# Up products of the gated layers as 512-column matmuls, and a quarter of their low weight parts by an adding transfer

## The chip, the cores and the metric

The kernel runs on one core of one Trainium2 chip. The metric is device time in microseconds (us), from the start to the end of one execution. A core has a matrix engine (TensorE, "PE" in the profile), whose weight loads the profile lists apart as "PEld", a vector engine (VectorE, "DVE"), a scalar engine (ScalarE, "ACT"), a general engine (GpSimd, "POOL") and SyncE ("SP"), which here only issues transfers. Each takes its instructions strictly in the order in which they were written, and an instruction that waits holds up all those behind it on its engine.

## The reference

The model has four layers of attention with a convolved, gated feed-forward part ("gated layers" here), and then one layer of another kind with two SwiGLU parts. All data are float32, 256 tokens of width 1024. The change touches the feed-forward part of the four layers:

```python
D_FF = 2752
CONV_W = 3

def conv_gated_ffn(h, w_up, conv_w, conv_b, w_down):
    u = h @ w_up
    C = u.shape[-1]
    u = lax.conv_general_dilated(u, conv_w[:, None, :].astype(u.dtype), window_strides=(1,),
                                 padding=[(CONV_W - 1, 0)], dimension_numbers=('NWC', 'WIO', 'NWC'),
                                 feature_group_count=C) + conv_b
    gate, val = jnp.split(u, 2, axis=-1)
    return (jax.nn.silu(gate) * val) @ w_down

for layer in range(DEPTH):
...
    h = rmsnorm(x, ffn_norm[layer])
    x = x + conv_gated_ffn(h, ffn_w_up[layer], ffn_conv_w[layer], ffn_conv_b[layer], ffn_w_down[layer])
```

## The kernel before

**Products.** Each float32 operand is split into a high part (the value rounded to float32r) and a low part (the rest), and a product is the sum of high x high, high x low and low x high. Activations lie feature-major, 128 features by 256 tokens, with both parts side by side in one tile (`act.hl`). `fm` (L191) runs over blocks of 128 x 128 weights. In its plain form a block is three matmuls of 256 columns (weight high by activation high, weight high by activation low, weight low by activation high), all summed in one half of a PSUM bank. In its wide form (`wide=True`) it is two: weight high by both activation parts as 512 columns, which fills a whole bank with two sums, and weight low by activation high as 256 columns. Whoever reads a wide result has to add the two halves.

**Weights.** They come in 282 chunks of 1 MB (`dma_to`, L128, on SP's queue, four `stage` buffers). A chunk is two units of 8 blocks. `split_next` (L152) makes the parts of a unit: ACT copies it to `whi` (L164), rounding, and DVE subtracts `whi` from the staged weights into `wlo` (L167), 128 x 1024 elements each. Both have five buffers. When PE's order reaches the fifth block of unit u, `take` (L170) has unit u + 4 split; the DVE instruction of it is written six blocks later, in these layers (`self.lag = 6`, `self.AHEAD = 4`). So `wlo` of a unit is written 22 blocks ahead of its first use.

**Order.** Nothing is scheduled by time. `tick` (L230) is called after each block and lets helpers (generators, `spawn`) write their next instructions once the block count (`self.pos`) has passed the number that they asked for. So the place of every ACT and DVE instruction is fixed by block counts, and the engines meet through semaphores.

**A gated layer** (`ffn_layer`, L767) multiplies 43 column tiles up, 8 blocks each: 21 pairs (a gate tile and its value tile) and one single tile that holds the two halves of the last 64 columns. The first pair and the single tile go together, and then 20 pairs follow, one after the other. Both tiles of a pair lie in one PSUM bank `u` (three of these; five others, `s`, serve attention). When a pair is done, `gate` (L788) is started for it. It writes, in this order: DVE multiplies both tiles by the norm factor `r` into `ub` (L792, 128 x 512); two blocks on, ACT starts both convolution sums `y` (L798); two on, DVE adds two taps of the first (L802); one on, ACT takes SiLU `gs` (L269) and DVE adds the taps of the second; four on, DVE multiplies to `g` (L814), ACT rounds it to `ghl` (L818); four on, DVE writes the low part (L825). All of that for one pair is written while PE's order is in the next pair, together with the splits of two units. The first gates wait for `r`, which comes only after the first blocks. The down product (22 units, wide) follows in the same order of the gated tiles.

The wide form with the adding of halves is what the SwiGLU parts use already (`swiglu`, L862, gate instructions L882 to L899): ACT copies the second halves (L882), DVE adds the first halves (L885), then DVE multiplies by `r` (L888).

Of the kernel before, what the change touches and what calls it, by code (L numbers as in the profile page):

```python
# [12 lines left out]
AF = mybir.ActivationFunctionType  # L13
OP = mybir.AluOpType
# [4 lines left out]
P = 128  # L19
T = 256  # L20
D = 1024
KT = 8
# [51 lines left out]
def up_cols(i):  # L74
    if i < 21:
        return [np.arange(128 * i, 128 * i + 128), np.arange(D_FF + 128 * i, D_FF + 128 * i + 128)]
    a = np.arange(128 * 21, D_FF)
    return [np.concatenate([a, D_FF + a])]
# [8 lines left out]
class Act:  # L87
# [3 lines left out]
    def __init__(self, hl, stacked=None):  # L91
        self.hl, self.h, self.l, self.done, self.stacked = hl, hl[:, 0], hl[:, 1], set(), stacked


class Net:
    def __init__(self, tc, ctx, A):
        self.tc = tc
        self.nc = tc.nc
        self.A = A
        self.side = []  # L100
        self.made = {}
        pool = lambda n, b, **k: ctx.enter_context(tc.tile_pool(name=n, bufs=b, **k))
        self.const = pool("const", 1)
        self.res = pool("res", 1)
        self.stage = pool("stage", 4)
        self.wsp = pool("wsp", 5)
        self.tmp = pool("tmp", 2)
        self.pu = pool("pu", 3, space=PSUM)
        self.psd = pool("psd", 5, space=PSUM)
        self.dram = pool("dram", 1, space=DRAM)  # L110
        self.rec = []
        self.pos = 0
        self.n_dma = 0
        self.n_split = 0
        self.chunks = {}
        self.wunits = {}
        self.AHEAD = 3
        self.acc = {}
        self.summed = {}
        self.late = None  # L120
        self.bt_bufs = 3
        self.lag = LAG[0]
        self.v_at = 5
# [29 lines left out]
    def split_next(self, step, lag=0):  # L153

        nc = self.nc
        i = self.n_split
        src = self.chunks[i // 2][:, (i % 2) * 1024:(i % 2) * 1024 + 1024]
        hi = self.wsp.tile([P, 1024], F32R, tag="whi", name="whi")
        lo = self.wsp.tile([P, 1024], F32R, tag="wlo", name="wlo")
        self.wunits[i] = (hi, lo)  # L160
        self.n_split += 1
        for o in range(0, 1024, step):
            s = slice(o, o + step)
            nc.scalar.activation(hi[:, s], src[:, s], AF.Copy)  # L164
            if lag:
                yield lag
            nc.vector.tensor_tensor(lo[:, s], src[:, s], hi[:, s].bitcast(F32), OP.subtract)  # L167
            yield 0
# [595 lines left out]
    def ffn_layer(self, layer, xf, nxt):  # L764
        nc = self.nc
        name = "ffn_w_up"
        cv = lambda i, part, tap: self.vec[:, CONV_COL + ((layer * 4 + tap) * N_UP + 2 * i + part):][:, 0:1]  # L767
        with ExitStack() as st:
            pool = st.enter_context(self.tc.tile_pool(name="ffn%d" % layer, bufs=2))
            gp = st.enter_context(self.tc.tile_pool(name="ffng%d" % layer, bufs=1))  # L770
            ga = Act(gp.tile([P, 2, 22, T], F32R, tag="ghl", name="ghl"), 21)
            gh, gl = ga.h, ga.l
            gz = gl[:, 21]
            self.zero(gz[64:])
            ub = [gp.tile([P, 2, 258], F32, tag="ub%d" % i, name="ub%d" % i) for i in range(3)]
            for t in ub:
                nc.gpsimd.memset(t[:, :, 0:2], 0.0)
            self.lag = 6
            self.AHEAD = 4
            self.start_norm(delay=27)  # L780
            order = [0, 21] + list(range(1, 21))
            lead = [up_cols(0), up_cols(21)]
            banks = [self.ubank(), self.ubank()]

            def gate(n, i, bank):

                np_ = len(up_cols(i))
                m = P if np_ == 2 else 64  # L788
                while self.r is None:
                    yield 1  # L790
                u = ub[n % 3]
                nc.vector.tensor_tensor(  # L792
                    u[:, 0:np_, 2:258], bank[:, 0:np_ * T].rearrange("p (a t) -> p a t", t=T),
                    self.r.unsqueeze(1).to_broadcast([P, np_, T]), OP.mult)
                yield 2
                y = pool.tile([P, 2, T], F32, tag="y", name="y")
                for p in range(np_):
                    nc.scalar.activation(y[:, p], u[:, p, 2:258], AF.Identity, scale=cv(i, p, 2), bias=cv(i, p, 3))  # L798

                def taps(p):  # L800
                    for tap in (1, 0):
                        nc.vector.scalar_tensor_tensor(y[:, p], u[:, p, tap:tap + T], cv(i, p, tap), y[:, p],  # L802
                                                       op0=OP.mult, op1=OP.add)
                yield 2
                taps(0)
                yield 1
                gs = pool.tile([P, T], F32, tag="gs", name="gs")
                self.silu(gs[:m], y[:m, 0])
                if np_ == 2:
                    taps(1)  # L810
                yield 4
                g = pool.tile([P, T], F32, tag="g", name="g")
                if np_ == 2:
                    nc.vector.tensor_tensor(g, gs, y[:, 1], OP.mult)  # L814
                else:
                    nc.scalar.activation(g[:64], y[64:128, 0], AF.Copy)
                    nc.vector.tensor_tensor(g[:64], gs[:64], g[:64], OP.mult)
                nc.scalar.activation(gh[:m, i], g[:m], AF.Copy)  # L818
                if np_ == 1:
                    nc.scalar.activation(gz[:64], g[:64], AF.Copy)  # L820
                if n == 21:
                    self.pin()
                yield 4
                low = gl[:, i] if np_ == 2 else gh[64:, i]
                nc.vector.tensor_tensor(low, g[:m], gh[:m, i].bitcast(F32), OP.subtract)  # L825
                ga.done.add(i)

            def start(n, i, bank, delay=0):
                gen = gate(n, i, bank)
                self.spawn(gen, delay or next(gen), ga)  # L830

            self.fm([(b[:, p * T:p * T + T], name, layer, cols, p == 0)
                     for b, parts in zip(banks, lead) for p, cols in enumerate(parts)], xf, range(KT))
            for n, i in enumerate(order):
                if n >= 2:
                    bank = self.ubank()
                    for p, cols in enumerate(up_cols(i)):
                        self.fm([(bank[:, p * T:p * T + T], name, layer, cols, True)], xf, range(KT))
                    start(n, i, bank)
                else:  # L840
                    start(n, i, banks[n], 8 * n)
            xn = self.new_act()
            rows = [np.arange(128 * kt, 128 * kt + 128) for kt in range(21)]
            rows.append(np.tile(np.arange(128 * 21, D_FF), 2))

            def after(c, ps):
                for n in range(2):
                    nc.vector.tensor_tensor(self.x[:, c], self.x[:, c], ps[:, n], OP.add)  # L848
                nxt(xn, c)

            self.down("ffn_w_down", layer, ga, order, after, rows)
            self.lag = 4
        return xn
# [607 lines left out]
```

## Time and profile before

| | us |
|---|---|
| median of 2 runs (1761.38 to 1761.99) | 1761.68 |
| profiled execution, its own time | 1761.36 |
| its span, first to last instruction | 1759.6 |
| PE busy | 1742.1 (99%) |
| DVE busy | 1404.4 (80%) |
| ACT busy | 1118.0 (64%) |
| POOL busy | 27.4 (2%) |

The profile is of one execution. Its own time stands 1.8 us above its span, and 0.3 us below the median. Busy time is a mean over stages; PE's counts pipelined matmuls with modelled ends, so 99% does not say that PE ran at its peak. The granted clock of TensorE over the whole is 0.995 of 2.4 GHz. The four gated layers' up products take about 124 us each.

### The profile page before, as it was taken

To read this page: it belongs to the slowest core of one execution; us is meant where nothing else is said; L and a number is where in the kernel's file an instruction comes from. 1 tells how busy PE (TensorE), PEld (TensorE's weight loads), DVE (VectorE), ACT (ScalarE), POOL (GpSimd) and SP (SyncE) were. 2 spreads that over 40 slices of the span, in tenths; PEclk is the share of its full clock that TensorE was granted. 3 is DMA by queue.
4 is the path that set the end of the run, shared out by engine and by line. 5 is a ranking of instruction groups with operands and counts; after the bars stand their busy time and mean duration, and the time that the engine had idled before them with its cause. 6 is when DMAs were issued, how large, how long until landed. Compare 5 with 4: busy or idle time off the path is not lost.

```text
span 1759.6 us, 31591 instructions
## 1 busy us (share of the span) xinstructions
PE 1742.1 (99%) x12556; PEld 1635.2 (93%) x12556; DVE 1404.4 (80%) x2582; ACT 1118.0 (64%) x1996; POOL 27.4 (2%) x67
## 2 busy tenths in 40 slices
PE   9999999999999999999999999999999999999998
PEld 8999998999999899999899999988888999988886
DVE  6989996897998688899689799868875767568763
ACT  6776664676766477666467766656655557466553
POOL 1000000000000000000000000000000020000000
PEclk9999999999999999999999999999999999999999
DMA  8735555434455553455554455555555544344551
GB/s 276 271 132 188 191 194 213 145 139 160 158 192 192 200 183 117 172 192 211 183 187 150 158 189 187 199 176 182 204 205 191 181 167 168 123 153 170 190 197 66
DMA packets 56212, 314.66 MB, mean 179 GB/s; under 512 B 5616, under 2 KB 18320, under 8 KB 20224
## 3 DMA queue, kind: packets, MB, share of 16 engines
q1 hardware_dynamic: 54720, 309.79, 49.1%
q8 instruction: 99, 1.62, 0.4%
q0 software_dynamic: 768, 2.09, 0.3%
q10 hardware_dynamic: 576, 0.75, 0.2%
q14 instruction: 49, 0.40, 0.1%
HBM read 311.52 MB, written 5.29 MB: 180 GB/s over the span
## 4 chain that ended last, share of the span: by engine, by line
PE 92%; DVE 5%; ACT 2%; issue 1%; DMA 0%; POOL 0%; DVEq 0%; ACTq 0%; POOLq 0%
PE u L185 80%; PE s L185 11%; DVE wlo L167 1%; DVE s L475 1%; PE s L492 1%; DMA oh<-onehot 0%; ACT s L266 0%; ACT whi L164 0%; DVE u L888 0%; DVE u L885 0%; ACT mt L280 0%; DVE mt L281 0%; POOL ps L1080 0%; DVE qs L422 0%; DVE s L638 0%
## 5 line engine op out<-in xcount | busy, mean ns | idle before, releaser
L185 PE MATMUL u<-xt,whi 128*128 128x256 f32 (+1 forms) x4352 | 861.1, 294 | 2.9 <-DVE xt L281 1.7
L167 DVE TENSOR_TENSOR wlo<-stage,whi 128x1024 fp32r<-128x1024 f32 (+1 forms) x568 | 681.4, 1212 | 71.8 <-ACT whi L164 69.0
L185 PEld LDWEIGHTS u<-xt,whi 128*128 128x128 f32 x4352 | 691.3, 192 | 22.0 <-issue 2.2
L185 PE MATMUL u<-xt,wlo 128*128 128x256 f32 x2352 | 665.2, 283 | 0.4 <-DVE wlo L167 0.4
L164 ACT ACTIVATE whi<-stage 128x1024 fp32r<-128x1024 f32 (+1 forms) x568 | 586.9, 1043 | 82.4 <-PE u L185 69.4
L185 PEld LDWEIGHTS u<-xt,wlo 128*128 128x128 f32 x2352 | 450.4, 192 | 1.3 <-DVE wlo L167 1.1
L185 PE MATMUL u<-ghl,whi 128*128 128x512 f32 x880 | 304.9, 389 | 0.0
L185 PE MATMUL u<-ghl,wlo 128*128 128x256 f32 x880 | 244.4, 279 | 0.0
L185 PEld LDWEIGHTS u<-ghl,whi 128*128 128x128 f32 x880 | 164.9, 187 | 37.7
L802 DVE SCALAR_TENSOR_TENSOR y<-ub,vec,y 128x256 f32<-128x256 f32 x344 | 159.6, 482 | 10.3 <-ACT y L798 3.3
L185 PEld LDWEIGHTS u<-ghl,wlo 128*128 128x128 f32 x880 | 165.0, 188 | 0.0
L185 PE MATMUL u<-o,whi 128*128 128x256 f32 x768 | 144.2, 287 | 1.1 <-DVE o L606 0.5
L798 ACT ACTIVATE y<-ub,vec 128x256 f32<-128x256 f32 x172 | 94.3, 594 | 58.7 <-DVE ub L792 58.7
L185 PE MATMUL s<-xt,whi 128*128 128x512 f32 x352 | 127.9, 399 | 0.0
L185 PEld LDWEIGHTS u<-o,whi 128*128 128x128 f32 x768 | 118.7, 189 | 4.0 <-issue 1.4
L185 PE MATMUL u<-o,wlo 128*128 128x256 f32 x384 | 108.1, 282 | 0.0
L185 PE MATMUL s<-xt,wlo 128*128 128x256 f32 x352 | 98.9, 281 | 0.0
L818 ACT ACTIVATE ghl<-g 128x256 fp32r<-128x256 f32 x88 | 36.9, 420 | 90.0 <-DVE g L814 88.0
L185 PE MATMUL u<-whi,xt 128*128 128x256 f32 (+1 forms) x448 | 90.2, 300 | 0.0
L363 ACT ACTIVATE xt<-x,vec 128x256 fp32r<-128x256 f32 x72 | 36.3, 504 | 83.1 <-DVE x L848 66.4
L185 PEld LDWEIGHTS s<-xt,whi 128*128 128x128 f32 x352 | 66.4, 189 | 15.6
L266 ACT ACTIVATE s<-s,nm 128x128 f32<-128x128 f32 x112 | 49.7, 445 | 48.7 <-DVE nm L480 48.7
(235 smaller groups left out, 2047.5 us busy)
## 6 DMA issues: line engine op xcount, KB each, us to landing
stage<-w SPq DMA_DIRECT2D x280, 1024.0 KB, 4.8
bt<-bt_d SPq DMA_DIRECT2D x24, 256.0 KB, 5.2
bt_d<-rows_d SPq DMA_DIRECT2D x1, 2048.0 KB, 12.2
stage<-w SPq DMA_DIRECT2D x4, 256.0 KB, 6.8
stage<-w SPq DMA_DIRECT2D x2, 512.0 KB, 8.9
bt_d<-rows_d SPq DMA_DIRECT2D x2, 512.0 KB
bt_d<-rows_d SPq DMA_DIRECT2D x1, 1024.0 KB
mem<-memT POOLq DMA_DIRECT2D x8, 128.0 KB, 2.9
```

Of the source, the lines that this page charges most:

```text
L164: nc.scalar.activation(hi[:, s], src[:, s], AF.Copy)
L167: nc.vector.tensor_tensor(lo[:, s], src[:, s], hi[:, s].bitcast(F32), OP.subtract)
L185: self.nc.tensor.matmul(out, lhsT, rhs, start=start, stop=stop, skip_group_check=True)
L266: self.nc.scalar.activation(out, in_, func, **kw)
L363: nc.scalar.activation(act.h[:, j], src, AF.Copy, scale=gcol)
L475: nc.vector.tensor_tensor_reduce(s[:, j, sl], ps[j][:, sl], bt[:, j, bs], 1.0, init(j), OP.add, OP.max, mx[:, 2 * j + t:2 * j + t + 1])
L492: self.nc.tensor.transpose(ps[:, o:o + 128], a[:, o:o + 128], self.ident)
L798: nc.scalar.activation(y[:, p], u[:, p, 2:258], AF.Identity, scale=cv(i, p, 2), bias=cv(i, p, 3))
L802: nc.vector.scalar_tensor_tensor(y[:, p], u[:, p, tap:tap + T], cv(i, p, tap), y[:, p], op0=OP.mult, op1=OP.add)
L818: nc.scalar.activation(gh[:m, i], g[:m], AF.Copy)
```

## The change

In the gated layers the up products use the wide form. A pair now takes two whole banks, the gate tile in `u` and the value tile in `s`. `gate` begins with the adding of halves: ACT copies the second half of each into `ub` (L800 of the changed kernel), a block later DVE adds the first halves (L803), and the product with `r` (L806) now reads and writes `ub`. While a layer's up blocks are written, every fourth unit gets its low part without DVE: ACT writes the rounded weights, negated, into `wlo` (L165), POOL issues a transfer that reads the unit's weights from DRAM again and adds them to `wlo` in SBUF (L166, 512 KB), and ACT then writes `whi` (L167).

```diff
@@ split_next
-        src = self.chunks[i // 2][:, (i % 2) * 1024:(i % 2) * 1024 + 1024]
+        cols = slice((i % 2) * 1024, (i % 2) * 1024 + 1024)
+        src = self.chunks[i // 2][:, cols]
...
+        if self.low_by_dma and i % self.low_by_dma == 0:
+            nc.scalar.activation(lo, src, AF.Copy, scale=-1.0)
+            nc.gpsimd.dma_start(out=lo, in_=self.A["w"][i // 2, :, cols], accum_op=OP.add)
+            nc.scalar.activation(hi, src, AF.Copy)
+            yield 0
+            return
@@ ffn_layer
             self.AHEAD = 4
+            self.low_by_dma = 4
...
-            banks = [self.ubank(), self.ubank()]
-
-            def gate(n, i, bank):
+            bank = lambda p: (self.sbank() if p else self.ubank()).rearrange("p (a t) -> p a t", a=2)
+
+            def gate(n, i, outs):
...
+                u = ub[n % 3]
+                for p, o in enumerate(outs):
+                    nc.scalar.activation(u[:, p, 2:258], o[:, 1], AF.Copy)
+                yield 1
+                for p, o in enumerate(outs):
+                    nc.vector.tensor_tensor(u[:, p, 2:258], o[:, 0], u[:, p, 2:258], OP.add)
                 while self.r is None:
                     yield 1
-                u = ub[n % 3]
-                nc.vector.tensor_tensor(
-                    u[:, 0:np_, 2:258], bank[:, 0:np_ * T].rearrange("p (a t) -> p a t", t=T),
-                    self.r.unsqueeze(1).to_broadcast([P, np_, T]), OP.mult)
+                nc.vector.tensor_tensor(u[:, 0:np_, 2:258], u[:, 0:np_, 2:258],
+                                        self.r.unsqueeze(1).to_broadcast([P, np_, T]), OP.mult)
                 yield 2
...
                 if n >= 2:
-                    bank = self.ubank()
-                    for p, cols in enumerate(up_cols(i)):
-                        self.fm([(bank[:, p * T:p * T + T], name, layer, cols, True)], xf, range(KT))
-                    start(n, i, bank)
+                    outs = [bank(p) for p in range(2)]
+                    for o, cols in zip(outs, up_cols(i)):
+                        self.fm([(o, name, layer, cols, True)], xf, range(KT), wide=True)
+                    start(n, i, outs)
...
             xn = self.new_act()
+            self.low_by_dma = 0
```

The fixed order moves with this. On ACT, in the middle of the first gated layer's up product, a pair's instructions before were these, from the rounding of one gated tile to the next (`ghl` L818, `whi` L164 a split, `y` L798 the convolution, `gs` L269 SiLU):

```order
L818 ACTIVATE ghl<-g 128x256
L164 ACTIVATE whi<-stage 128x1024
L798 ACTIVATE y<-ub_1771,vec 128x256 x2
L164 ACTIVATE whi<-stage 128x1024
L269 ACTIVATE gs<-y 128x256
L818 ACTIVATE ghl<-g 128x256
```

In the changed kernel the same stretch, over two pairs, reads as follows (`ghl` is now L831, `whi` L172, `y` L811, `gs` L277; L165 and L167 are the unit whose low part comes by transfer; L800 are the copies of second halves):

```order
L831 ACTIVATE ghl<-g 128x256
L172 ACTIVATE whi<-stage 128x1024
L800 ACTIVATE ub_1772<-u 128x256
L800 ACTIVATE ub_1772<-s 128x256
L811 ACTIVATE y<-ub_1772,vec 128x256 x2
L172 ACTIVATE whi<-stage 128x1024
L277 ACTIVATE gs<-y 128x256
L831 ACTIVATE ghl<-g 128x256
L165 ACTIVATE wlo<-stage 128x1024
L167 ACTIVATE whi<-stage 128x1024
L800 ACTIVATE ub_1770<-u 128x256
L800 ACTIVATE ub_1770<-s 128x256
```

The two copies stand behind the split that follows `ghl`, and in every second pair behind two full-width ACT instructions.

On DVE a pair before was this, from one gated tile `g` (L814) to the next (`wlo` L167 a split, `ghl` L825 the low part, `ub` L792 the product with `r`, `y` L802 the taps):

```order
L814 TENSOR_TENSOR g<-gs,y 128x256
L167 TENSOR_TENSOR wlo<-stage,whi 128x1024
L825 TENSOR_TENSOR ghl<-g,ghl 128x256
L792 TENSOR_TENSOR ub_1770<-u,r 128x2x256
L167 TENSOR_TENSOR wlo<-stage,whi 128x1024
L802 SCALAR_TENSOR_TENSOR y<-ub_1770,vec,y 128x256 x4
L814 TENSOR_TENSOR g<-gs,y 128x256
```

In the changed kernel, over the same two pairs as on ACT (L803 adds the halves, L806 multiplies by `r`, L815 are the taps, L827 is `g`, L175 a split, L838 the low part):

```order
L803 TENSOR_TENSOR ub_1772<-u,ub_1772 128x256
L803 TENSOR_TENSOR ub_1772<-s,ub_1772 128x256
L806 TENSOR_TENSOR ub_1772<-ub_1772,r 128x2x256
L175 TENSOR_TENSOR wlo<-stage,whi 128x1024
L815 SCALAR_TENSOR_TENSOR y<-ub_1772,vec,y 128x256 x4
L827 TENSOR_TENSOR g<-gs,y 128x256
L175 TENSOR_TENSOR wlo<-stage,whi 128x1024
L838 TENSOR_TENSOR ghl<-g,ghl 128x256
L803 TENSOR_TENSOR ub_1770<-u,ub_1770 128x256
L803 TENSOR_TENSOR ub_1770<-s,ub_1770 128x256
L806 TENSOR_TENSOR ub_1770<-ub_1770,r 128x2x256
L815 SCALAR_TENSOR_TENSOR y<-ub_1770,vec,y 128x256 x4
```

Two adds stand ahead of the product with `r`, and in every second pair the split between that product and the taps is gone. In the first and third gated layer the transferred unit falls where it stands here, between `ghl` and the copies on ACT; in the second and fourth it falls between `y` and `gs` on ACT, and the split that goes on DVE is the one behind `g`. Over the steps from the third gated tile of a layer to its last, 19 of them, 9 hold a transferred unit in the first, second and fourth layer and 10 in the third. POOL's order gains 43 transfers (11, 10, 11 and 11 in the four layers); SP's is unchanged.

## Rows read from the trace of the kernel before

**Rows 1.** Page, chain of work that ended last: shares of the span by line
```profile
PE u L185 80%; PE s L185 11%; DVE wlo L167 1%; DVE s L475 1%; PE s L492 1%; DMA oh<-onehot 0%; ACT s L266 0%; ACT whi L164 0%; DVE u L888 0%; DVE u L885 0%; ACT mt L280 0%; DVE mt L281 0%; POOL ps L1080 0%; DVE qs L422 0%; DVE s L638 0%
```
**Rows 2.** Windows, first up product: length; busy of PE, PEld, DVE, ACT, POOL; clock, DMA share, GB/s
```profile
150.00:245.00 95.00, 95.00 (x794) 95.00 (x793) 91.98 (x155) 64.10 (x102) 0.00 (x0) 1.00 0.52 186
```
**Rows 3.** Timeline of DVE, one pair: start us, length us, instructions
```profile
195.72 1.22 DVE L167 TENSOR_TENSOR wlo<-stage,whi 128x1024 fp32r<-128x1024 f32 x1
196.86 0.42 DVE L825 TENSOR_TENSOR ghl<-g,ghl 128x256 fp32r<-128x256 f32 x1
197.20 0.68 DVE L792 TENSOR_TENSOR ub<-u,r 128x512 f32<-128x512 f32 x1
197.80 1.21 DVE L167 TENSOR_TENSOR wlo<-stage,whi 128x1024 fp32r<-128x1024 f32 x1
198.93 1.92 DVE L802 SCALAR_TENSOR_TENSOR y<-ub,vec,y 128x256 f32<-128x256 f32 x4
200.95 0.42 DVE L814 TENSOR_TENSOR g<-gs,y 128x256 f32<-128x256 f32 x1
201.29 1.22 DVE L167 TENSOR_TENSOR wlo<-stage,whi 128x1024 fp32r<-128x1024 f32 x1
```
**Rows 4.** Timeline of ACT, the same pair: in brackets the idle time before
```profile
197.97 1.09 ACT L798 ACTIVATE y<-ub,vec 128x256 f32<-128x256 f32 x2 [0.76 <-DVE ub L792]
198.97 1.04 ACT L164 ACTIVATE whi<-stage 128x1024 fp32r<-128x1024 f32 x1
199.96 0.42 ACT L269 ACTIVATE gs<-y 128x256 f32<-128x256 f32 x1
201.41 0.42 ACT L818 ACTIVATE ghl<-g 128x256 fp32r<-128x256 f32 x1 [1.03 <-DVE g L814]
201.73 1.04 ACT L164 ACTIVATE whi<-stage 128x1024 fp32r<-128x1024 f32 x1
```
**Rows 5.** Timeline of DVE and PE, first gated layer: third and last `g`, first down matmul
```profile
150.85 0.43 DVE L814 TENSOR_TENSOR g<-gs,y 128x256 f32<-128x256 f32 x1
...
256.62 0.42 DVE L814 TENSOR_TENSOR g<-gs,y 128x256 f32<-128x256 f32 x1
...
251.73 0.39 PE L185 MATMUL u<-ghl,whi 128*128 128x512 f32 x1
```
**Rows 6.** Chain in order of time, first SwiGLU: one tile of 8 wide blocks
```profile
1251.61 2.77 PE u L185 x16
```
**Rows 7.** Timeline of ACT, first SwiGLU: a split and the copies of second halves
```profile
1249.17 1.05 ACT L164 ACTIVATE whi<-stage 128x1024 fp32r<-128x1024 f32 x1
1250.12 0.36 ACT L882 ACTIVATE u<-u 128x256 f32<-128x256 f32 x1
1250.38 0.38 ACT L882 ACTIVATE u<-s 128x256 f32<-128x256 f32 x1
```
**Rows 8.** Timeline of DVE, first SwiGLU: adds, product with `r`, split
```profile
1245.87 0.42 DVE L885 TENSOR_TENSOR u<-u 128x256 f32<-128x256 f32 x1
1246.20 0.42 DVE L885 TENSOR_TENSOR u<-s,u 128x256 f32<-128x256 f32 x1
1246.65 0.69 DVE L888 TENSOR_TENSOR u<-u,rr 128x512 f32<-128x512 f32 x1
1247.26 1.22 DVE L167 TENSOR_TENSOR wlo<-stage,whi 128x1024 fp32r<-128x1024 f32 x1
```
**Rows 9.** Page, DMA issues: count, KB each, median us from issue to landing
```profile
stage<-w SPq DMA_DIRECT2D x280, 1024.0 KB, 4.8
...
bt_d<-rows_d SPq DMA_DIRECT2D x1, 2048.0 KB, 12.2
...
mem<-memT POOLq DMA_DIRECT2D x8, 128.0 KB, 2.9
```
**Rows 10.** Windows, the kernel's start; columns as in rows 2
```profile
5.00:10.00 5.00, 2.42 (x8) 0.87 (x7) 1.57 (x4) 2.15 (x5) 2.40 (x5) 0.79 1.01 322
10.00:15.00 5.00, 5.00 (x14) 3.90 (x13) 4.11 (x9) 3.68 (x10) 0.00 (x0) 0.53 1.04 393
```

More of the change, by code (lines that the diff above doesn't have):

```diff
@@ L826, in gate, with start @@
                 ga.done.add(i)
-            def start(n, i, bank, delay=0):
-                gen = gate(n, i, bank)
+            def start(n, i, outs, delay=0):
+                gen = gate(n, i, outs)
                 self.spawn(gen, delay or next(gen), ga)
-            self.fm([(b[:, p * T:p * T + T], name, layer, cols, p == 0)
-                     for b, parts in zip(banks, lead) for p, cols in enumerate(parts)], xf, range(KT))
+            first = [[bank(p) for p in range(len(parts))] for parts in lead]
+            self.fm([(o, name, layer, cols, True) for outs, parts in zip(first, lead) for o, cols in zip(outs, parts)],
+                    xf, range(KT), wide=True)
             for n, i in enumerate(order):
                 if n >= 2:
-                    bank = self.ubank()
-                    for p, cols in enumerate(up_cols(i)):
-                        self.fm([(bank[:, p * T:p * T + T], name, layer, cols, True)], xf, range(KT))
-                    start(n, i, bank)
+                    outs = [bank(p) for p in range(2)]
+                    for o, cols in zip(outs, up_cols(i)):
+                        self.fm([(o, name, layer, cols, True)], xf, range(KT), wide=True)
+                    start(n, i, outs)
                 else:
-                    start(n, i, banks[n], 8 * n)
+                    start(n, i, first[n], 8 * n)
             xn = self.new_act()
+            self.low_by_dma = 0
             rows = [np.arange(128 * kt, 128 * kt + 128) for kt in range(21)]
```

## The prediction, made before the changed kernel was run

> **What bounds the kernel now.** I read the chain of waits first. PE's products make 80% + 11% of it [rows 1], and a late low weight part (`wlo`) 1%: the matrix engine sets the time almost everywhere. So the question is what the up product lets PE do, and I went to the windows of that stage. In 95 us of it PE is busy throughout at clock 1.00, but DVE is busy for 91.98 us and ACT for 64.10 [rows 2]. PE did 794 matmuls there, three to a block: 95 / 794 x 3 = 0.359 us a block, 5.74 us a pair of tiles. DVE's own pace is in its timeline: from one split behind `g` (195.72) to the next (201.29) it takes 5.57 us, and each of its instructions starts when the one before it lets it; there is no idle time in the pair [rows 3]. DVE is thus 0.17 us a pair faster than PE, and no more. ACT idles 0.76 us before `y` and 1.03 us before `ghl`, both times waiting for DVE [rows 4]. It is a loop between two engines in fixed order: `g` (DVE) releases `ghl` (ACT), the product with `r` (DVE) releases `y` (ACT), `y` releases the taps (DVE). At present the loop's waits all fall on ACT, which has time.
>
> How far DVE is ahead of PE at the end: in the first gated layer the last `g` starts at 256.62 [rows 5]; the split behind it (0.34 later, 1.22 long, as in rows 3) ends at 258.18. It is the unit that PE needs 32 blocks into the down product, which begins at 251.73 [rows 5] and runs wide, at 2.77 / 8 = 0.347 us a block [rows 6]: at 262.8. So DVE has 4.6 us in hand there. I take that for all four layers.
>
> **What the change removes and adds.**
>
> PE: a wide block takes 0.347 us against 0.359, so 344 up blocks give up to 344 x 0.012 = 4.1 us a layer, 16.5 us in all. That counts only if PE still sets the pace.
>
> DVE, per pair: two adds, the first 0.33 us before the next, the second 0.45 us before the product with `r`, which waits for its result [rows 8]: +0.78. That product reads SBUF in place of PSUM, 0.69 against 0.68 [rows 3, 8]: nothing. Half a split, as one unit in four goes: -1.13 / 2 = -0.57 [rows 3]. Sum 5.57 + 0.78 - 0.57 = 5.78 us a pair, if DVE never waits. That is over PE's 5.74 of before and over the 16 x 0.347 = 5.55 that PE could now do.
>
> ACT, per pair: two copies, 0.26 us between their starts and 0.38 us for the second, some 0.6 [rows 7], and half a full-width instruction, 0.5 [rows 4]: of 1.79 idle us it keeps about 0.7.
>
> But the loop closes differently. The copies stand on ACT behind `ghl` and a split, that is behind DVE's `g`; the adds on DVE wait for the copies; behind the adds stand the product with `r`, a split, the taps and the next `g`; and behind all of these waits PE, for `wlo`. I follow it from a start of `g` at 0, with the steps between starts in rows 3, 4, 7 and 8.
>
> Step without a transferred unit. ACT: `ghl` 0.46, `whi` 0.78 (200.95, 201.41, 201.73 in rows 3 and 4), first copy 0.95 later at 1.73, ending at 2.09. DVE: split at 0.34, low part at 1.48, free at 1.82; the add waits until 2.13 (handoff 0.04, as from `g` to `ghl`). Then second add 2.46, product 2.91, split 3.52, taps 4.65, next `g` 2.02 later: 6.67 us.
>
> Step with one, first and third layer. ACT writes `wlo` at 0.78, `whi` at 1.73, and the copy at 2.68, ending at 3.04. DVE adds at 3.08 and 3.41, multiplies at 3.86 to 4.55. No split follows, so the taps wait for `y`: it starts 0.09 after the product (197.88 to 197.97), lasts 0.59 (two, 0.50 apart, last 1.09), and the taps start at 5.27. Next `g`: 7.29 us.
>
> Step with one, second and fourth layer. As the first kind up to the product (2.91 to 3.60); `y` 3.69, `wlo` 4.69, `whi` 5.64, `gs` only at 6.63, ending at 7.05; `g` waits for it: 7.09 us. The split that went on DVE leaves a hole there, as the add still waits for the copies.
>
> Nineteen steps: first layer 10 x 6.67 + 9 x 7.29 = 132.3; third, 9 and 10, 132.9; second and fourth, 10 x 6.67 + 9 x 7.09 = 130.5 each. Before they took 256.62 - 150.85 = 105.8 [rows 5]. Ahead of the third `g` stand three adds on the path, 0.45 + 0.33 + 0.45 = 1.2. What a layer loses is then 1.2 + its sum - 105.8 - 4.6 (what DVE had in hand): 23.1, 21.3, 23.7 and 21.3, together 89 us. PE can run at most 22 blocks ahead of DVE, so its faster blocks turn into waiting, and the 16.5 us are not seen. The sum against the profiled execution: 1761.4 + 89 = **1851 us** (the median shown is 0.3 us above that execution).
>
> The transfers: 512 KB each, adding in SBUF, which the trace doesn't show. From below, 2.9 us, a quarter of the size on the same queue; from above, 12.2 us, the slowest landing [rows 9]. I take 3.7, in proportion to size between 2.9 (128 KB) and 4.8 (1024 KB), the rows nearest in kind. Such a unit is wanted by PE about when the unit ahead of it is done, one tile (2.8 us) after its own negative copy or later, and a late one only delays PE within waits that it has anyhow, until it delays the unit behind the last `g`. At 3.7 it doesn't. At 12.2 it lands 8.5 later and costs up to 8 us in each layer, some 30. The gain from below is nothing, as DVE sets the pace. The extra traffic, 0.5 MB beside 2 MB of weights, meets a DMA share of 0.52 [rows 2]: no bound.
>
> A rule that speaks against these transfers: the Trainium skill ("SBUF — State Buffer", section "SBUF: two separate sides") says that a transfer issued from GpSimd waits for its descriptors while VectorE holds a shared port in a two-port mode. If it struck here, DVE being busy nearly always, the transfers would land late, and by the bound above the sum would be 1881. The same skill ("VectorE: DVE Perf Modes", section "Why `tensor_tensor` can't do 2×_2P or 4×") takes two-tensor instructions out of that mode. No run here shows it yet.
>
> **The rivals.**
> - *DVE alone sets the pace*, ACT's waits not showing: the copies are done before DVE asks. For it: ACT keeps 0.7 us a pair. Against: the order has the copies behind `ghl`. Then 19 x 5.78 = 109.8, and a layer loses 1.2 + 109.8 - 105.8 - 4.6 = 0.6: 1764 us, not slower. It decides below 6.2 us a step: 35 us (2%) / 4 = 8.8 = 1.2 + 19 p - 105.8 - 4.6 gives p = 6.2.
> - *PE sets the pace*, the change doing what it could: 1761.4 - 16.5 = 1745 us. It needs 5.55 us a step, and DVE's bare work is above.
> - *Late transfers*: as the forecast, and 12 us from issue to landing, 1881 us.
> - *The clock falls.* In 5 to 10 us PE had 8 matmuls and was busy 2.42 of 5 us; the granted clock went to 0.79, and in the 5 us behind to 0.53 before it came back [rows 10]. Now PE will wait some 1.2 to 1.4 us a pair. At the 1.2 GHz level throughout, a pair would need 2 x 5.55 = 11.1 us, 76 steps x (11.1 - 6.9) = 320 us more: about 2170. Against: a PE that is 80% busy is far above those 2.42 of 5, and while it falls for a few us the loop hides it. The Trainium skill ("TensorE: Matmul & The Clock Gate", section "Part 1: The HAM clock gate") has idleness halve the clock and activity restore it; the trace's start agrees with its 0.53.
>
> **How the numbers follow.** Forecast 0.79; late transfers 0.07; clock 0.02; DVE alone 0.08; PE 0.03; 0.01 for a gain that I don't see. A measurement tells about 2% (35 us) from no change: slower 0.79 + 0.07 + 0.02 = 0.88, within 2% 0.08 + 0.03 = 0.11, faster 0.01. The range is 1797 to 1885. Its low end is a step of 6.2 us, which an overlap that I missed could bring; its high end has the transfers' upper bound on the forecast. Outside lie the two cases without a loss (0.11), the clock and a little of the late transfers, under 0.2 together.
>
> **What would show it.** Right: in the up product PE waits for `wlo`, released by DVE; DVE's add waits about 0.3 us for ACT's copy in plain steps and 1.3 to 2 us in steps with a transferred unit; steps of 6.7 and 7.1 to 7.3 us in turn, `g` to `g`; DVE's busy share in that stage falls below the 0.97 of now though its work grows; a wide block with all inputs there takes 0.347. Wrong: PE not waiting in the stage; steps near 5.8; PE waiting mainly for transfers, which would put the loss there; a granted clock below 1.00 in the stage.

## The result, and the profile after

The changed kernel takes 1873.19 us (two runs, 1871.23 and 1875.15) against 1761.68 before: 1.0621 times as long, 95% interval 1.0593 to 1.0649. The forecast was 1851, the range 1797 to 1885.

The page's chain of waits is the first thing to set beside [rows 1]. By engine, PE had 92% of it and now has 61%; DVE and ACT had 7% together and now hold 31%. The first line is the kernel before, the other two the change.

```profile
PE 92%; DVE 5%; ACT 2%; issue 1%; DMA 0%; POOL 0%; DVEq 0%; ACTq 0%; POOLq 0%
...
PE 61%; DVE 19%; ACT 12%; DMA 4%; issue 3%; POOL 0%; SPq 0%; DVEq 0%; ACTq 0%; POOLq 0%
PE u L193 49%; PE s L193 12%; DVE y L815 6%; DVE wlo L175 3%; ACT whi L172 3%; DVE ub L803 3%; DVE ub L806 2%; ACT wlo L165 2%; DMA wlo<-w 2%; ACT whi L167 2%; DVE g L827 2%; ACT y L811 1%; ACT ub L800 1%; ACT ghl L831 1%; DMA bt<-bt_d 1%
```

The window of the first up product (columns as in [rows 2]) shows every engine with idle time. PE is busy for 87% of it where it was busy throughout, DVE for 81% where it was 97%, although DVE has more to do.

```profile
150.00:275.00 125.00, 108.70 (x579) 93.03 (x578) 100.95 (x188) 84.73 (x154) 7.85 (x9) 0.95 0.65 182
```

Where three engines all wait in the same stretch, a loop between them is a likely cause. The chain in order of time (start us, length us, piece; "issue" is time in which the engine waited for nothing that the profile shows) shows it piece by piece for one plain step, `g` to `g`:

```profile
187.71 0.44 DVE g L827
188.14 0.02 issue
188.17 0.02 ACT ghl L831
188.19 0.30 issue
188.49 1.05 ACT whi L172
189.54 0.27 ACT ub L800
189.81 0.02 issue
189.83 0.77 DVE ub L803 x2
190.60 0.02 issue
190.62 0.69 DVE ub L806
191.32 1.14 DVE wlo L175
192.45 0.41 DVE y L815
192.86 0.03 issue
192.88 0.89 DVE y L815 x2
...
194.39 0.44 DVE g L827
```

There is neither a PE piece nor a transfer in it: `g`, `ghl`, a split, the copies, the adds, the product with `r`, a split, the taps, `g`. From 187.71 to 194.39 it takes 6.68 us.

DVE's timeline of the next two steps (the pieces that matter; [rows 3] is the same stretch before) shows where DVE waits: 1.18 us for the copy and 0.73 for `y` in the step with a transferred unit, 0.23 for the copy in the plain one.

```profile
194.39 0.43 DVE L827 TENSOR_TENSOR g<-gs,y 128x256 f32<-128x256 f32 x1
...
197.47 0.43 DVE L803 TENSOR_TENSOR ub<-u,ub 128x256 f32<-128x256 f32 x1 [1.18 <-ACT ub L800]
...
199.68 1.92 DVE L815 SCALAR_TENSOR_TENSOR y<-ub,vec,y 128x256 f32<-128x256 f32 x4 [0.73 <-ACT y L811]
201.71 0.42 DVE L827 TENSOR_TENSOR g<-gs,y 128x256 f32<-128x256 f32 x1
...
203.84 0.42 DVE L803 TENSOR_TENSOR ub<-u,ub 128x256 f32<-128x256 f32 x1 [0.23 <-ACT ub L800]
...
208.39 0.42 DVE L827 TENSOR_TENSOR g<-gs,y 128x256 f32<-128x256 f32 x1
```

The steps are 7.32 and 6.68 us. The transfers, of which the trace before had none, take 7.5 us from issue to landing at the median (page, DMA issues, beside the weights' own row, which stayed as in [rows 9]):

```profile
stage<-w SPq DMA_DIRECT2D x280, 1024.0 KB, 4.8
wlo<-w POOLq DMA_DIRECT2D x43, 512.0 KB, 7.5
```

And PE names them. Groups of the page: busy us, mean ns | idle us before, and what ended it.

```profile
L193 PE MATMUL u<-xt,wlo 128*128 128x256 f32 x1680 | 480.1, 286 | 33.1 <-DMA wlo<-w 32.2
...
L193 PE MATMUL s<-xt,wlo 128*128 128x256 f32 x1024 | 294.2, 287 | 41.4 <-DMA wlo<-w 41.3
...
L193 PE MATMUL u<-ghl,wlo 128*128 128x256 f32 x880 | 246.3, 281 | 9.2 <-DMA wlo<-w 9.2
```

So PE waits 82.7 us for transfers there, and 1.0 us for anything else. Two readings are open. By the chain, DVE and ACT set the pace and the transfer is only the last thing that PE is missing (theory A of the runs). By PE's own waits, the transfers set it (theory B). The prediction had the first and named the second as a sign against itself.

### The profile page after: what moved, and what is told of

Read it like the earlier page. It is cut to its first block, busy times and chain, and to the rows that moved or that the text cites. A ratio compares the mean times of both kernels' runs of the same rounds, so it can differ in the third digit from the quotient of the medians.

```text
span 1873.4 us, 29289 instructions
## 1 busy us (share of the span) xinstructions
PE 1763.3 (94%) x11180; PEld 1579.5 (84%) x11180; DVE 1432.4 (76%) x2711; ACT 1204.0 (64%) x2211; POOL 64.9 (3%) x110
## 4 chain that ended last, share of the span: by engine, by line
PE 61%; DVE 19%; ACT 12%; DMA 4%; issue 3%; POOL 0%; SPq 0%; DVEq 0%; ACTq 0%; POOLq 0%
PE u L193 49%; PE s L193 12%; DVE y L815 6%; DVE wlo L175 3%; ACT whi L172 3%; DVE ub L803 3%; DVE ub L806 2%; ACT wlo L165 2%; DMA wlo<-w 2%; ACT whi L167 2%; DVE g L827 2%; ACT y L811 1%; ACT ub L800 1%; ACT ghl L831 1%; DMA bt<-bt_d 1%
## 5 line engine op out<-in xcount | busy, mean ns | idle before, releaser
L175 DVE TENSOR_TENSOR wlo<-stage,whi 128x1024 fp32r<-128x1024 f32 (+1 forms) x525 | 629.7, 1213 | 72.3 <-ACT whi L172 69.5
L193 PE MATMUL u<-xt,whi 128*128 128x256 f32 (+1 forms) x2304 | 627.5, 342 | 3.1 <-DVE xt L289 1.9
L172 ACT ACTIVATE whi<-stage 128x1024 fp32r<-128x1024 f32 (+1 forms) x525 | 542.3, 1043 | 89.4 <-PE u L193 68.7
L193 PE MATMUL u<-xt,wlo 128*128 128x256 f32 x1680 | 480.1, 286 | 33.1 <-DMA wlo<-w 32.2
L193 PEld LDWEIGHTS u<-xt,whi 128*128 128x128 f32 x2304 | 399.1, 192 | 54.5 <-DVE xt L289 2.7
L193 PE MATMUL s<-xt,whi 128*128 128x512 f32 x1024 | 378.3, 404 | 0.0
L193 PEld LDWEIGHTS u<-xt,wlo 128*128 128x128 f32 x1680 | 324.4, 193 | 40.1 <-DMA wlo<-w 37.9
L193 PE MATMUL s<-xt,wlo 128*128 128x256 f32 x1024 | 294.2, 287 | 41.4 <-DMA wlo<-w 41.3
L193 PEld LDWEIGHTS s<-xt,wlo 128*128 128x128 f32 x1024 | 198.7, 194 | 47.6 <-DMA wlo<-w 47.0
L193 PEld LDWEIGHTS s<-xt,whi 128*128 128x128 f32 x1024 | 197.2, 193 | 46.0
L815 DVE SCALAR_TENSOR_TENSOR y<-ub,vec,y 128x256 f32<-128x256 f32 x344 | 159.4, 483 | 26.7 <-ACT y L811 19.8
L811 ACT ACTIVATE y<-ub,vec 128x256 f32<-128x256 f32 x172 | 94.3, 594 | 103.0 <-DVE ub L806 103.0
L831 ACT ACTIVATE ghl<-g 128x256 fp32r<-128x256 f32 x88 | 36.8, 418 | 72.9 <-DVE g L827 68.3
```

The source lines that it names most:

```text
L193: self.nc.tensor.matmul(out, lhsT, rhs, start=start, stop=stop, skip_group_check=True)
```

## The experiments

Each was timed against the kernel before on the same chip. Where a table speaks of steps, they are read from DVE's timeline as the time between starts of `g`; "19 steps" is from the third to the last `g` of a layer, "gap" from a layer's last `g` to the third of the next.

**Wide products without transfers.**

```diff
-            self.low_by_dma = 4
+            self.low_by_dma = 0
```

> The wide up products alone; every low weight part again by VectorE, no transfer. Theory A (the loop VectorE g, ScalarE ghl, ScalarE split, ScalarE copies, VectorE adds sets the pace of the up stage): every step from one g to the next is a plain one, 6.7 us, 19 of them 127 us against 105.8 before, and with the 1.2 us later start 22.3 us a layer: 1851 us; 1833 if VectorE had 4.6 us a layer in hand. Theory B (TensorE waits for the transfers, which land after 7.5 us, and they set the pace): without transfers no step is longer than before, 1745 to 1764 us.

Measured 1837.49 us, 1.0417 (1.0393 to 1.0440). Every step is 6.68 or 6.69 us, 127.0 a layer in all four. Without a single transfer most of the loss is there, which is A and not B. The time lies between A's two figures, nearer to the one with DVE's 4.6 us in hand.

**Transfers with the products of before.** The same lines of `split_next` and `ffn_layer` put into the kernel before, `gate` as it was.

> The narrow gate and products of before, and only every fourth unit's low part by the adding transfer. Theory A (loop of VectorE and ScalarE through the copies): there are no copies, so steps stay within 0.1 us of 5.57 and the time within 1755 to 1790 us, the upper end if the last transferred unit of a layer lands late by up to 5 us. Theory B (transfers set the pace): most of the loss stays, 1840 us or more, with TensorE waiting for each transferred unit.

Measured 1788.55 us, 1.0142 (1.0117 to 1.0166), the upper end of A in time; its steps within 0.1 us of 5.57 did not come. From the fifth step of the first layer on the steps run mostly 6.07 and 5.45 in turn, 5.76 on average, and PE is busy for 59.8 of 60 us in 200 to 260: with DVE relieved, PE's own 16 blocks of 0.36 us are the bound, and there is nothing to win behind DVE.

**The whole change without the transfer.**

```diff
-            nc.gpsimd.dma_start(out=lo, in_=self.A["w"][i // 2, :, cols], accum_op=OP.add)
```

> The whole change without the transfer itself: ScalarE still writes the negated copy, VectorE still leaves the unit out, but nothing is added to the copy, so the low part of every fourth unit is left at minus the high part (that part of the computation is changed). Theory A: the steps stay 6.7 and 7.3 (7.0 in layers 2 and 4), and only what the late landings cost on top goes: 1850 to 1866 us. Theory B: TensorE no longer waits, 1745 to 1770 us.

Measured 1854.00 us, 1.0521 (1.0489 to 1.0554). This settles A against B: but for single ones, the steps are as in the change to a hundredth (7.32 and 6.68 in the first layer, 7.04 and 6.68 in the second). Three starts of `g` in the first layer:

```profile
187.98 0.43 DVE L826 TENSOR_TENSOR g<-gs,y 128x256 f32<-128x256 f32 x1
...
195.30 0.43 DVE L826 TENSOR_TENSOR g<-gs,y 128x256 f32<-128x256 f32 x1
...
201.98 0.43 DVE L826 TENSOR_TENSOR g<-gs,y 128x256 f32<-128x256 f32 x1
```

PE still waits 66.7 us in the same three groups of its page, 62.4 of them now for DVE:

```profile
L192 PE MATMUL u<-xt,wlo 128*128 128x256 f32 x1680 | 479.6, 285 | 37.6 <-DVE wlo L174 37.6
...
L192 PE MATMUL s<-xt,wlo 128*128 128x256 f32 x1024 | 292.9, 286 | 23.1 <-DVE wlo L174 18.9
...
L192 PE MATMUL u<-ghl,wlo 128*128 128x256 f32 x880 | 246.4, 281 | 6.0 <-DVE wlo L174 5.9
```

PE's waits moved from one releaser to the other (82.7 to 62.4 us in all), the pace did not. What the transfer itself costs is 1.0621 - 1.0521 = 0.0100 of 1762, some 18 us (10 to 25 by the two intervals).

**`g` later in the order**, so that on ACT the next pair's copies stand ahead of `ghl`.

```diff
-                yield 4
+                yield 4 if n == 21 else 12
                 g = pool.tile([P, T], F32, tag="g", name="g")
```

> The whole change, with g and its two followers written 8 blocks later (the last gate as it was), so that on ScalarE the copies of the next pair stand ahead of the rounding of g and no longer wait for it. Theory A: the loop through g is cut; a plain step falls to VectorE's own work, about 6.35 us, one with a transferred unit to about 6.9 (through gs, two copies of a split, the copies of the next pair, adds, y, first taps): some 6.5 us a layer less than the change, 1835 to 1860 us. Theory B: transfers are untouched, 1868 to 1878 us.

Measured 1840.25 us, 1.0436 (1.0409 to 1.0463): 33 us gone by the order alone, with the same instructions and the same transfers. Steps are 6.71 and 6.10 us (6.17 in the second and fourth layer), 0.2 under what A gave. B has no explanation for a change.

**The transfers without the wide products, and without the transfer itself**, that is transfer_only less its `dma_start`.

> As transfer_only (narrow products, every fourth unit's low part not by VectorE), but without the transfer itself: the low part stays minus the high part (that part of the computation is changed). Transfer_only was 24.5 us above the kernel before with steps of 5.76 us on average, which is TensorE's 16 blocks of 0.36 us. If its loss is the late landing, 1755 to 1768 us here, as before; if it is ScalarE's two copies in a row, 1780 to 1792 us.

Measured 1762.67 us, 0.9994 (0.9980 to 1.0009). So ACT's two copies in a row cost nothing there, and the 25 us of transfer_only are late landings. There they cost time in the middle of a layer: the 19 steps of the four layers take 439.1 us with the transfer and 418.3 without, the gaps 550.2 and 550.5. It also shows that DVE's relief alone brings nothing: 10 or 11 splits a layer less on DVE, and the same time, since PE is the bound.

**No transfers near the end of a layer.**

```diff
             for n, i in enumerate(order):
+                if n == 17:
+                    self.low_by_dma = 0
```

> The whole change, but from the 18th pair of a layer on VectorE makes the low parts again: 10 of the 43 transfers go, the last two or three of each layer. If the 19 us that the transfer costs (the change against no_transfer) are paid at the end of a layer, where the last ones land late, some 14 us go, and 4 us more by the shorter steps: 1852 to 1859 us. If they are paid by TensorE's waits throughout the stage, 10 of 43 of 19 and those 4: 1863 to 1869 us.

Measured 1850.07 us, 1.0500 (1.0479 to 1.0521), a little better than the first case. The gaps say where it went:

| | 19 steps, four layers (us) | three gaps, sum (us) |
|---|---|---|
| before | 423.5 | 546.3 |
| the change | 526.4 | 546.7 |
| no_transfer | 526.7 | 537.1 |
| no_last_transfers | 522.0 | 537.0 |
| wide_only | 508.0 | 536.8 |

Without the last two or three transfers of a layer the gaps are those of no transfer at all. With wide products the transfers in the middle of a layer cost no time, for all of PE's waiting; the last cost 9.7 / 3 = 3.2 us a layer. The fourth layer, which has no gap behind it, shows it too: from a layer's last `g` to the end of its down product it is 51.5 to 51.6 us in every layer of wide_only, no_transfer and no_last_transfers, and 55.9, 53.3, 55.3 and 56.0 in the change, 14 us more in the four. PE's timeline at the first layer's last one, issued at 280.52, shows it:

```profile
285.01 0.39 PE L193 MATMUL u<-ghl,whi 128*128 128x512 f32 x1
288.54 0.38 PE L193 MATMUL u<-ghl,wlo 128*128 128x256 f32 x1 [3.15 <-DMA wlo<-w]
...
290.39 0.63 PE L193 MATMUL u<-ghl,whi 128*128 128x512 f32 x1
```

Here nothing else is seen to hold PE up: it is in the down product, and the other matmul of the same block, with the same `ghl`, has run at 285.01. Behind the wait it has lost 3.15 us, and a wide matmul takes 0.63 us instead of 0.39. The windows around it (busy of PE first, clock third from the end) show what PE did before: 1.85 of 5 us busy, and then a mean granted clock of 0.67, between the levels of 1.2 and 2.4 GHz.

```profile
280.00:285.00 5.00, 5.00 (x32) 4.44 (x31) 3.02 (x7) 3.67 (x8) 0.88 (x1) 1.00 0.74 215
285.00:290.00 5.00, 1.85 (x11) 1.40 (x10) 4.59 (x9) 2.89 (x8) 0.00 (x0) 0.99 0.81 193
290.00:295.00 5.00, 5.00 (x21) 4.27 (x21) 4.11 (x8) 3.94 (x7) 0.00 (x0) 0.67 0.33 125
```

**A transfer that overwrites.**

```diff
-            nc.gpsimd.dma_start(out=lo, in_=self.A["w"][i // 2, :, cols], accum_op=OP.add)
+            nc.gpsimd.dma_start(out=lo, in_=self.A["w"][i // 2, :, cols])
```

> The whole change, with the transfer overwriting instead of adding (the low part of every fourth unit becomes the whole weight: that part of the computation is changed). If the adding makes the landing 7.5 us long, it falls to 3 to 5 us and the time to that of no_transfer, 1850 to 1858 us; if it is the queue, the size or the traffic of the other transfers, the landing stays at 6.5 us or more and the time at 1868 to 1878 us.

Measured 1862.12 us, 1.0569 (1.0539 to 1.0599), between the two cases. The landing, shortest, median and longest (it was 5.4/7.5/10.7 in the change):

```profile
DMA to landing us min/median/max: 4.0/5.6/8.3
```

So the adding is 1.9 of the 7.5 us. What makes the other 5.6, the queue, descriptors that had to wait, the size or the traffic, these runs don't tell apart.

**Wide, without transfers, the halves added by GpSimd**, and `y` of a pair written behind the copies of the next.

```diff
+                both = pool.tile([P, 2, 2, T], F32, tag="both", name="both")
...
-                    nc.scalar.activation(u[:, p, 2:258], o[:, 1], AF.Copy)
+                    nc.scalar.activation(both[:, p], o, AF.Copy)
...
-                    nc.vector.tensor_tensor(u[:, p, 2:258], o[:, 0], u[:, p, 2:258], OP.add)
+                    nc.gpsimd.tensor_tensor(u[:, p, 2:258], both[:, p, 0], both[:, p, 1], OP.add)
+                yield 1 if n == 21 else 9
...
-                yield 2
+                yield 2 if n == 21 else 8
                 y = pool.tile([P, 2, T], F32, tag="y", name="y")
```

> Towards a version better than both: wide products, no transfers, ScalarE copies both halves, GpSimd adds them (0.74 to 1.02 us each by its rows of 128x256, two a pair), and y of a pair is written behind the copies of the next, so that no loop goes through the copies. Theory A (the loop and VectorE's added work made the loss): VectorE has 5.57 us a pair, as before, TensorE 16 x 0.347 = 5.55: steps 5.6 us and 1745 to 1768 us. Rival: GpSimd's adds stall VectorE for as long as they run, up to 2 us a pair: steps 7.2 to 7.6 us, 1870 to 1910 us.

Measured 1819.75 us, 1.0340 (1.0312 to 1.0368): neither. Steps are 6.42 us. DVE now waits for little (it is busy for 96.05 of 100 us in its window, columns as in [rows 2]), but its work is not 5.57: its taps are longer beside GpSimd (last section).

```profile
170.00:270.00 100.00, 90.85 (x499) 76.14 (x500) 96.05 (x140) 72.17 (x124) 42.61 (x32) 1.00 0.47 166
```

**Wide, without transfers, `g` later**: the edits of wide_only and of late_g together.

> Wide products, no transfers, and g written 8 blocks later as in late_g: the loop through the copies is cut and no transfer lands late. If the loss of wide_only (steps of 6.68 us) is VectorE's added work plus a loop of 0.33 us, the step falls to VectorE's own work, 5.57 + 0.78 = 6.35 us, and the time by 4 x 19 x 0.33 = 25 us under wide_only: 1806 to 1820 us. If another wait takes the loop's place, the steps stay at 6.6 to 6.7 and the time at 1832 to 1842 us.

Measured 1802.06 us, 1.0223 (1.0199 to 1.0247), faster than expected. The steps are 6.17 us and DVE is busy for 98.28 of 100 us (first line, the window), without a wait in its timeline:

```profile
170.00:270.00 100.00, 96.09 (x521) 79.13 (x519) 98.28 (x179) 67.78 (x131) 0.00 (x0) 1.00 0.48 169
...
203.82 0.42 DVE L827 TENSOR_TENSOR g<-gs,y 128x256 f32<-128x256 f32 x1
204.16 1.22 DVE L175 TENSOR_TENSOR wlo<-stage,whi 128x1024 fp32r<-128x1024 f32 x1
205.29 1.00 DVE L815 SCALAR_TENSOR_TENSOR y<-ub,vec,y 128x256 f32<-128x256 f32 x2
206.20 0.42 DVE L838 TENSOR_TENSOR ghl<-g,ghl 128x256 fp32r<-128x256 f32 x1
206.54 1.00 DVE L815 SCALAR_TENSOR_TENSOR y<-ub,vec,y 128x256 f32<-128x256 f32 x2
207.46 1.22 DVE L175 TENSOR_TENSOR wlo<-stage,whi 128x1024 fp32r<-128x1024 f32 x1
208.59 0.42 DVE L803 TENSOR_TENSOR ub<-u,ub 128x256 f32<-128x256 f32 x1
...
209.99 0.42 DVE L827 TENSOR_TENSOR g<-gs,y 128x256 f32<-128x256 f32 x1
```

It is 0.18 under my 6.35, since the late order also saves DVE a wait for its own results: from the first of four taps to `g` was 2.02 us [rows 3]; now two pairs of taps take 0.91 and 0.92 from start to start, with other work right behind each. So of wide_only's step, 6.68, DVE's work is 6.17 and the order is 0.51: 0.18 of it that wait for its own results, the other 0.33 the loop. It is the best of the wide versions, and its DVE is still slower than the 5.76 us that PE needs with narrow products.

**The same, with the low part of `g` on GpSimd.**

```diff
-                nc.vector.tensor_tensor(low, g[:m], gh[:m, i].bitcast(F32), OP.subtract)
+                nc.gpsimd.tensor_tensor(low, g[:m], gh[:m, i].bitcast(F32), OP.subtract)
```

> The same with the low part of g (one subtraction of 128x256 a pair, 0.34 us on VectorE) on GpSimd. If GpSimd works beside VectorE at no cost, a step is 6.01 us and the time 26 us less than wide_late_g, 1780 to 1794 us. If VectorE's taps are stretched while GpSimd runs, as the taps of adds_on_gpsimd (0.69 us each beside GpSimd's 2.67 us a pair, 0.48 us in the kernel before), 0.83 us for 2.67 us of GpSimd or 0.4 us for one subtraction of 1.3 us: nothing is won, 6.3 to 6.45 us a step, 1804 to 1822 us.

Measured 1811.38 us, 1.0273 (1.0248 to 1.0299), and steps of 6.32: the second case. DVE is rid of 0.34 us a pair, and a step is longer by 0.15. No version here beats the kernel before.

## Why the prediction was right, and where not

**The pace of the stage: right, step by step.** The prediction built three steps out of single instructions: 6.67 us plain, 7.29 with a transferred unit in the first and third layer, 7.09 in the others. The trace has 6.68, 7.32 and 7.04. Nineteen steps were forecast at 132.3, 130.5, 132.9 and 130.5 and took 132.7, 130.2, 133.3 and 130.2: together 526.4 against 423.5 before, 103 us of the 111.5 lost. Not all of it is the loop. An estimate: DVE's added work of 0.78 us in each of the 76 steps makes 59 us, the loop in plain steps (wide_only's 508.0) 25 more, and the longer steps with a transferred unit the last 18. late_g and wide_late_g show that the order is a cause and not only the place, as moving one yield changes the time by 33 to 35 us; part of that, 0.18 of 0.51 us a step, is DVE's wait for its own results.

**What stands around the steps: right without transfers.** The terms were a start later by 1.2 us a layer and 4.6 us that DVE had in hand, net 3.4 us gained a layer. The gaps of wide_only and no_transfer are 9.5 and 9.2 us shorter than before for three layers, 3.1 each. no_transfer, at 1854.0, is what the forecast's 1851 describes: the change, with a transfer that costs nothing. The 4.6 us in hand were well read: from the last `g` to the end of the down product it was 55.7 to 56.0 us before and is 51.5 to 51.6 there.

**The step that failed: "I take 3.7"**, the landing of the adding transfer, in proportion to size between two rows of plain transfers. It is 7.5, of which the adding is 1.9. The prediction said that a late landing costs nothing until it delays the unit behind a layer's last `g`, and this held with wide products: by no_last_transfers the late landings cost time there, 14 us in the four layers. But at 7.5 us it does delay it, and the time that DVE had in hand is used up (the change's gaps, 546.7, are again those of before, 546.3). The rival of late transfers had 12 us of landing and 1881; the result, 1873, is the forecast with a part of that rival on top, and with some 8 us that come from elsewhere (last paragraph of this section).

**A sign that was read wrongly: "PE waiting mainly for transfers, which would put the loss there".** PE did wait for them, 82.7 us, and for `wlo` from DVE hardly at all. The loss was not there. PE's wait carries the name of what came last; without the transfer the next in line, DVE's `wlo`, ends waits of 62.4 us, and the steps stay as they are. The same holds for the second wrong sign, a clock below 1.00 in the stage: it is 0.95 in the first layer, and 1.00 in no_transfer's window of 150 to 270 us, with the same steps.

```profile
150.00:270.00 120.00, 103.86 (x555) 84.40 (x553) 98.33 (x181) 81.50 (x148) 0.00 (x0) 1.00 0.41 145
```

The dips come with the single long waits for a transfer, and the loop hides them, but for those in the down product.

**PE's faster blocks: right that they are not seen.** A wide block took 0.35 us as in [rows 6], and PE stood idle for 13% of the stage.

**DVE's terms: too large by 0.18.** The +0.78 of the adds is real, but DVE's 5.57 held 0.19 us in which `g` waited for the taps' results. That mattered for none of the times forecast, as the steps were built from rows that hold this wait, and the change's order keeps it.

**The transfers' own gain, -0.57 us a pair of DVE work, is worth nothing in either form.** With narrow products PE is the bound (narrow_no_transfer, 0.9994); with wide ones the place of the split in the loop is taken by ACT's second copy, and a step with a transferred unit is longer than a plain one by 0.64 or 0.36 us.

One difference between the profiles is no part of this: in the first layer's attention, which the change doesn't touch and which comes before the first transfer of the new kind (140.2 us), DVE waits 8.2 us for a bias table in the change's profiled execution.

```profile
60.49 0.29 DVE L483 CUSTOM_DVE_ANT_0 s<-s,bt 128x128 f32<-128x128 f32 x1 [8.19 <-DMA bt<-bt_d]
```

Such a wait is 0 in that of before, 3.1 in no_transfer's, 7.8 in late_g's and 5.8 in wide_late_g's, which has no transfer of the new kind. What makes it long or short stays open, and so does how much of it is in the executions that were not profiled; some of the 18 us between the change and no_transfer may be this wait. The spans then add up: 102.9 us in the steps, 0.4 in the gaps, 8.9 ahead of the first layer's third `g`, with that wait in it, and 1.6 behind the last `g` are the 113.8 between 1759.6 and 1873.4.

## What to carry to other kernels

When several engines are idle in the same stretch, follow the chain in order of time through one period: a loop shows as one engine's name after the other, and its length can be worked out beforehand from the order of the instructions and the start-to-start times of the trace. The releaser of a wait is only the last of several; ask what would end the same wait if that one were early, before the loss is put down to it. And work taken off an engine is worth nothing where another engine is the bound or where it was filling a hole in a loop.

## What the runs showed of the hardware that was not expected

An adding transfer of 512 KB lands after 7.5 us and takes POOL 0.88 us to issue; overwriting, 5.6 and 0.53 (medians). The Trainium skill ("DMA: Bandwidth & Descriptors", section "Anatomy of one DMA — SWDGE (gpsimd) path") has a fit of 2.0 us and 436 KB a microsecond for this path, by which an estimate is 3.2 us; the runs have more than that for both kinds.

GpSimd beside DVE makes DVE's taps up to twice as long. One tap in the stage, shortest, median and longest in ns, without GpSimd (wide_late_g), beside its adds (adds_on_gpsimd) and beside its low parts (wide_late_g_low_gpsimd):

```profile
L815 DVE SCALAR_TENSOR_TENSOR y<-ub,vec,y x66: 476/484/490, 169.5 to 268.7; 128x256 f32<-128x256 f32 x66
```
```profile
L817 DVE SCALAR_TENSOR_TENSOR y<-ub,vec,y x61: 471/486/974, 171.7 to 270.0; 128x256 f32<-128x256 f32 x61
```
```profile
L815 DVE SCALAR_TENSOR_TENSOR y<-ub,vec,y x64: 476/485/969, 171.0 to 267.7; 128x256 f32<-128x256 f32 x64
```

In the window of adds_on_gpsimd the 30 taps that overlap an add take 0.84 to 0.97 us, and the other 31 at most 0.49. A split of 128x1024 on DVE never takes over 1.223 us in these windows, though 16 of them overlap an add, and the subtractions of 128x256 on DVE that overlap one keep their 0.42. GpSimd itself needs 1.35 us (mean) for one add and 1.20 for one subtraction of 128x256, where DVE needs 0.42. The Trainium skill ("SBUF — State Buffer", section "Who interferes with whom") says that a DVE instruction with two inputs in SBUF contends with one of GpSimd that reads SBUF. The taps agree; the splits, which have two such inputs as well, don't show it, with the reserve that GpSimd's spans in a profile are rough.
